# Accumulating transfers of two MLPs issued later: a hold moved to a form's last tile, block sums a group later

## The chip, the cores and the metric

The kernel runs on one core of a Trainium2 chip. The metric is the device time of one execution in microseconds. The core has five engines with a queue of instructions each: TensorE (PE in the profile; its weight loads are PEld), VectorE (DVE), ScalarE (ACT), GpSimd (POOL) and SyncE (SP). SP and POOL also issue the transfers (DMA) between the main memory and the on-chip buffer; an accumulating transfer, which adds what it brings to what lies at its destination, is issued by POOL.

## What is computed

Two layers on a sequence of 512 tokens of width 1024, in float32. Layer 0 has an attention mixer, layer 1 a gated short convolution; behind each stands an MLP with a causal convolution of width 3 between its up projection and its gate.

```python
def conv_ffn(h, norm_g, w_up, conv_w, w_down):      # D_FF = 2816, w_up: 1024 x 5632, w_down: 2816 x 1024
    xn = rms_norm(h, norm_g)
    u = causal_dwconv(xn @ w_up, conv_w)
    g, val = u[..., :D_FF], u[..., D_FF:]
    return (jax.nn.silu(g) * val) @ w_down

def short_conv_mixer(h, norm_g, w_in, conv_w, w_out):
    xn = rms_norm(h, norm_g)
    proj = xn @ w_in
    gate_b, gate_c, u = proj[..., :1024], proj[..., 1024:2048], proj[..., 2048:]
    return (gate_b * causal_dwconv(gate_c * u, conv_w)) @ w_out

for layer in range(2):
    h = h + (attention_mixer if layer % 2 == 0 else short_conv_mixer)(h, ...)
    h = h + conv_ffn(h, ...)
```

## The kernel before

The large products are computed as Strassen-like products of blocks: a product of 2 x 2 blocks takes seven block products, called forms, in place of eight: p1, p7, p2, p6, p3, q5 and q4. Each form multiplies a sum or difference of weight blocks with a sum or difference of activation blocks. Each float32 operand is split into an upper and a lower half (`whi` and `wlo` for weights; ACT rounds the upper one, VectorE subtracts it for the lower one), and three matmuls, hi by hi, lo by hi and hi by lo, give one product.

**Up projections** (class `Sevens`, used for both MLPs and, under the name `c`, for the conv stage's input). The columns are taken in groups `g` of 256. `slot(g, s)` records the work of form `s` of group `g`; the seven slots of a group follow each other. Four blocks of weights, named X, Y, W and Z, are loaded by SP. Sums of them are made by accumulating transfers on POOL (`add_block`): one into X in each group, and in the MLPs one into the tile `three`, which is the operand of forms p6 (before the transfer) and q4 (behind it). X as changed is the operand of q5. `tail(p, s)` does, within the slots of group `g`, the convolution and gate of the group before, `p = g - 1`; in slot 5 it calls `blocks.product`, where VectorE makes the gated activations. These lie in tiles `head_blocks`, `hs_b_blocks` and `hs_a_blocks`, in four quarters a, b, c and d of the down projection's operand. For rows that are complete according to the list `SUMS`, `product` also issues on POOL the block sum, an accumulating transfer within the on-chip buffer that adds quarter a to quarter b (256 or 128 KB).

**Conv stage.** It has groups 0 to 4, of which 1, 2 and 3 are listed in `aside`. In groups 0 and 4 VectorE adds X to Y in place (`first_sums`, kept as `self.summed`); the addition to X on POOL must wait for that, since it changes X. `join` (kept as `self.joined`) subtracts two results on VectorE.

**Down projections** (`mlp`). There are 7 forms by 6 tiles of weights (`GROUPS`: tiles of 2, 2, 2, 1, 2 and 2 blocks of 128 rows), 42 steps in the order p1, p7, p2, p6, p3, q5, q4. `want_sum` lists the tiles, and `bring` issues their transfers, two steps ahead. Tiles of p2 and p3 are plain loads into the three buffers `raw`. Those of the other forms lie in `_chain` tiles: `one(g)` (X_chain, Y_chain, p_hi_chain, p_lo_chain) serves p1 and then q5; `two(g)` (p_hi, p_lo, q_hi, q_lo, q_hi, q_lo with the ending `_chain`) serves p7, p6 and q4 in turn, and the accumulating transfer for the next form can start when the halves of the form before have been split. For q5's last three tiles SP loads a tile `other` into a `raw` buffer and VectorE adds it (line 291).

**What sets the order.** Each queue runs in the order in which it stands. A scheduler places the recorded instructions by their dependences, `pin` (`tc.keep_in_program_order`) keeps an instruction at the place where it was recorded, and `behind(later, earlier)` orders two instructions of one engine. All accumulating transfers stand on POOL's one queue. With an entry in `landed`, `bring` puts a small POOL operation `hold` ahead of a transfer, which reads one column of another tile and so waits until that has landed:

```python
if i in landed:
    hold, other = tiny.tile(...), raws[landed[i]][:, 0:1]
    held_ = pool.tensor_tensor(hold, other, other, op=ALU.add)
    behind(added, held_)
```

The only entry is that of the first MLP (`layer == 0`): the transfer of q4's tile 3 waits for p3's tile 3. Those of tiles 4 and 5 stand behind it.

Of the kernel before, what the change touches and what calls it, by code (L numbers as in the profile page):

```python
# [57 lines left out]
def trunk(  # L58
# [1005 lines left out]
    class Blocks:  # L1064
# [1 line left out]
        SUMS = (0, 2), (2, 4), (4, 6), (6, HEAD), (HEAD, 8), (8, 10), (10, HF)  # L1066

        def __init__(self, place, layer):
            self.layer, self.place, self.parts = layer, place, {}

        def at(self, j, n):
            start = 0 if j < HEAD else HEAD if j < HF else HF
# [9 lines left out]
        def product(self, j, n, g, u):  # L1082
            if n == 2 and j in (HEAD - 1, HF - 1):
                for i in range(2):
                    self.product(j + i, 1, g[:, i:i + 1, :], u[:, i:i + 1, :])
                return
            to = self.at(j, n)
            plus, minus = (LEFT, RIGHT) if j < HF else (RIGHT, LEFT)
            dve.tensor_tensor(to[:, :, plus], g[:, :, plus], u[:, :, plus], op=ALU.mult)
            dve.scalar_tensor_tensor(to[:, :, minus], g[:, :, minus], -1.0, u[:, :, minus], op0=ALU.mult, op1=ALU.mult)  # L1090
            for k0, k1 in self.SUMS:
                if j + n == k1:
                    tc.keep_in_program_order(
                        nc.gpsimd.dma_start(self.block("b", k0, k1 - k0), self.block("a", k0, k1 - k0), accum_op=ALU.add))

    def seven(acc, w, x, fresh, last=True):

# [9 lines left out]
    class Sevens:  # L1107
# [89 lines left out]
        def slot(self, g, s):  # L1197

            on, was, soon = (i in self.groups for i in (g, g - 1, g + 1))
            if self.chores:  # L1200
                self.work_off(self.rate(g, s))
            form, n, fresh = (("p1", "A", True), ("p7", "T", True), ("p3", "R", False), ("p6", "R", False), ("p2", "A", False),
                              ("q5", "R", False), ("q4", "T", False))[s]
            if s == 2:
                if was:
                    self.product(g - 1, form, n, fresh)
            elif on:
                self.product(g, form, n, fresh)
            st, p, c = self.st, g - 1, self.st.get(g)
            if s == 0:  # L1210
                if was:
                    if "p3" not in st[p]:
                        self.weights_of(p, "p3", "Z")
                    self.join(p, "yg", st[p]["T"], st[p]["Xs"])
                if on:
                    self.load_one(g, "W", self.block_of(g, 1, 0))
                if soon:
                    self.load_pair(g + 1)
            elif s == 1:
                first = not was  # L1220
                if on and first and not self.ahead and "p6" not in c:
                    self.weights_of(g, "p6", self.sum_of(g))
                if on and not first and self.table:
                    self.weights_of(g, "p6", "three")
                if on:
                    act.activation(self.bank_of(g, "R"), c["A"], AF.Copy, scale=-1.0)
                if on and not first and not self.table:
                    self.weights_of(g, "p6", self.sum_of(g))
                if on and first and self.name == 0:
                    self.weights_of(g, "p2", "W")  # L1230
                if soon and not self.table:
                    self.add_block(g + 1, "Y", 1, 1)
            elif s == 2:
                if on:
                    self.kept(g, "P7s", c["T"])
                    if "p2" not in c:
                        self.weights_of(g, "p2", "W")
                    c["four"] = c[self.sum_of(g)]
                    if self.table and soon:
                        self.add_block(g, "four", 1, 0)  # L1240
                    else:
                        dve.tensor_tensor(c["four"], c["four"], c["W"], op=ALU.add)
            elif s == 3:
                if was:
                    self.early(p, st[p]["R"])
                if on:
                    self.weights_of(g, "q5", "X")
                    if not self.table:
                        self.kept(g, "Xs", c["R"])
                        self.weights_of(g, "q4", "four")  # L1250
                        self.fourth = self.rest
            elif s == 4:
                if on and self.table:
                    self.kept(g, "Xs", c["R"])
                    self.weights_of(g, "q4", "four")
            if was and s != 2:
                self.tail(p, s)
            if s == 5:
                if on:
                    self.load_one(g, "Z", self.block_of(g, 1, 1))  # L1260
                    self.open_wides(g)
                    if soon and not self.table:
                        self.weights_of(g + 1, "p1", "X")
                        if g + 1 in self.aside:
                            self.three_of(g + 1)
                    self.left(g, c["A"])
                if soon and self.table:
                    self.weights_of(g + 1, "p1", "X")
                elif on and self.ahead and not soon:
                    self.weights_of(g, "p3", "Z")  # L1270
            elif s == 6:
                if on:
                    self.join(g, "yv", c["R"], c["P7s"])
                if soon:
                    self.first_sums(g + 1)
# [17 lines left out]
    def up_begin(layer, norm, mp, place):  # L1293

        blocks = Blocks(place, layer)
        if place is mp:
            blocks.at(0, 1)
        w_up, base = ffn_w_up[layer], PLAIN[layer]

        def block_of(g, kh, half):  # L1300
            c0 = half * DFF + 2 * g * P
            return w_up[kh * 512:(kh + 1) * 512, c0:c0 + 2 * P].rearrange("(k p) c -> p k c", p=P)

        up = Sevens(layer, mp, range(base, HF), block_of)
        up.norm, up.chores = norm, []
        up.table = lambda n, g: table_of(layer, n, g)
        up.scaled = not base
        up.rate = lambda g, s: 1.4 if g == base else 0.3 if layer else 0.5

        def wides_of(g):  # L1310
            if g == base - 1:
                t = hsp.tile([P, 8, S], F32, tag="hs_a", name=f"hs_a_wide{layer}")
                return {n: t[:, 2 * i:2 * i + 2, :] for i, n in enumerate(("yg", "yv", "ug", "uv"))}
            t = {n: mp.tile([P, 2, S], F32, tag=n, name=f"{n}{layer}{g}", bufs=1) for n in ("yg", "yv", "ug", "uv")[0 if place is mp else 2:]}
            if place is not mp:
                both = place.tile([P, 4, S], F32, tag="four", name=f"y_both{layer}{g}")
                t.update(yg=both[:, 0:2, :], yv=both[:, 2:4, :])
            return t
        up.wides_of = wides_of
        wides = up.wides  # L1320

        def taps_of(g, half, i):
            return lambda j: ffn_tap(layer, j, half * NF + 2 * g + i)

        def conv(g, half, i):
            src, dst = (wides[g][n[half]] for n in (("yg", "yv"), ("ug", "uv")))
            causal_conv(dst[:, i, :], src[:, i, :], taps_of(g, half, i))

        def tail(p, s):
            if s < 2:  # L1330
                conv(p, 0, s)
            elif s == 3:
                act.activation(wides[p]["ug"], wides[p]["ug"], AF.Silu)
                conv(p, 1, 0)
            elif s == 4:
                conv(p, 1, 1)
            elif s == 5:
                blocks.product(2 * p, 2, wides[p]["ug"], wides[p]["uv"])
        up.tail, up.conv = tail, conv
        return blocks, up  # L1340

# [230 lines left out]
    def mlp(layer, norm, mp, begun_up=None):  # L1572
# [25 lines left out]
        for name in PHASES:  # L1598
            for g, (k0, nk) in enumerate(GROUPS):
                if name in ("p2", "p3"):  # L1600
                    want_sum(lambda: None, nk, 512, block(1, 0 if name == "p2" else 1, k0, True), queue=pool if name == "p2" and g > 2 else None)
                elif name in ("p1", "q5"):
                    want_sum(
                        one(g), nk, 512, block(0, 0 if name == "p1" else 1, k0, name == "p1"), queue=dve if name == "q5" and g > 2 else None)
                elif name == "p7":
                    want_sum(two(g), nk, 512, block(0, 1, k0, True), block(1, 1, k0, False))
                else:
                    want_sum(two(g), nk, 512, block(0 if name == "p6" else 1, 0, k0, False))
        if layer == 0:
            landed[begun + 6 * len(GROUPS) + 3] = begun + 4 * len(GROUPS) + 3  # L1610
            want_conv()
        else:
            aside.update(range(begun, len(wanted)))
# [251 lines left out]
```

## Time and profile before

| | |
|---|---|
| median of 3 runs | 1103.2 us (1102.69 to 1106.39) |
| profiled execution | 1104.69 us, its span 1102.6 us |
| mean granted TensorE clock | 0.998 |
| busy share | TensorE 99%, its weight loads 93%, VectorE 87%, ScalarE 62%, GpSimd 16% |
| HBM | 205.72 MB read, 44.04 MB written |

The busy share of TensorE comes from matmuls whose ends are modelled and overlap; the number of matmuls that start in a stretch shows more. In rows of busy time by stretch, each engine has its busy us and in brackets its count of instructions (PE, PEld, DVE, ACT, POOL), then the granted clock, the share of the 16 DMA engines and GB/s. In rows in order of time, the columns are start and duration in us, engine, line, operation, written tile and read tiles; in square brackets stands the engine's idle time before it and what ended that. Rows of transfers give count, size and the us from issue to landing.

### The profile page before, as it was taken

The page shows a single profiled execution, that of the slowest core. Times are in us where ns is not written, and L with a number is a line of the kernel's source. Part 1 is how long each engine was busy: PE and PEld are TensorE (multiplying, and loading weights), DVE is VectorE, ACT ScalarE, POOL GpSimd, SP SyncE. Part 2 cuts the span into 40 slices and gives each one's busy share as a digit, 9 for nine tenths or more (in the row PEclk, how much of TensorE's full clock was granted, in tenths as well). Part 3 has the DMA queues.
Part 4 walks back from the last instruction along what each step waited for, and adds up shares of the span by engine and source line. Part 5 has one row for each costly group of instructions (what it writes and reads, how often), then busy time and mean ns, then how long its engine had stood idle before and what let it go on. Part 6 is the DMA issues. An engine that isn't in the chain of part 4 may idle for free.

```text
span 1102.6 us, 21693 instructions
## 1 busy us (share of the span) xinstructions
PE 1086.4 (99%) x8781; PEld 1030.7 (93%) x8781; DVE 959.3 (87%) x1483; ACT 685.3 (62%) x1021; POOL 181.0 (16%) x207
## 2 busy tenths in 40 slices
PE   9999999999999999999999999999999999999998
PEld 7888787879999999999989899999999999999998
DVE  5788898997899788899978889887899999999886
ACT  7466667655466676776546756456566657567653
POOL 4011111111012211114310101001112221014300
PEclk9999999999999999999999999999999999999999
DMA  7677778688667888899963775698879988899951
GB/s 198 166 189 193 187 178 221 173 211 230 190 163 207 198 195 222 210 268 212 232 170 92 193 180 134 135 260 211 212 182 220 209 202 184 222 269 203 240 150 58
DMA packets 178116, 214.21 MB, mean 194 GB/s; under 512 B 7676, under 2 KB 143916, under 8 KB 178016
## 3 DMA queue, kind: packets, MB, share of 16 engines
q0 software_dynamic: 53280, 95.34, 44.7%
q1 hardware_dynamic: 124576, 117.42, 33.4%
q8 instruction: 69, 1.13, 0.4%
q14 instruction: 31, 0.25, 0.1%
q10 hardware_dynamic: 160, 0.07, 0.0%
HBM read 205.72 MB, written 44.04 MB: 227 GB/s over the span
## 4 chain that ended last, share of the span: by engine, by line
PE 66%; DVE 16%; issue 10%; DMA 5%; ACT 3%; POOL 0%; DVEq 0%; ACTq 0%; POOLq 0%
PE psb L357 15%; PE psb L1102 15%; PE psb L1741 7%; PE psa L1741 7%; PE psa L1102 6%; PE psa L357 4%; DMA three<-in_ffn_w_up 4%; DVE wlo_p L1053 3%; DVE wlo L334 2%; PE psb L733 2%; PE psa L830 2%; ACT whi L333 1%; PE psc L357 1%; PE psc L805 1%; PE psb L615 1%
## 5 line engine op out<-in xcount | busy, mean ns | idle before, releaser
L1102 PE MATMUL psb<-p_hi,wlo_p 128*128 128x256 f32 x480 | 132.5, 276 | 1.0 <-DVE wlo_p L74 1.0
L1102 PE MATMUL psb<-p_hi,whi_p 128*128 128x256 f32 x480 | 132.6, 276 | 0.0
L1102 PE MATMUL psb<-p_lo,whi_p 128*128 128x256 f32 x480 | 132.6, 276 | 0.0
L333 ACT ACTIVATE whi<-raw 128x1024 fp32r<-128x1024 f32 (+2 forms) x77 | 79.0, 1027 | 68.7 <-PE psb L357 25.6
L334 DVE TENSOR_TENSOR wlo<-raw,whi 128x1024 fp32r<-128x1024 f32 (+2 forms) x77 | 90.9, 1180 | 24.5 <-ACT whi L333 24.3
L357 PE MATMUL psb<-hs_a,whi 128*128 128x512 f32 (+1 forms) x312 | 93.3, 369 | 0.0
L1102 PEld LDWEIGHTS psb<-p_hi,wlo_p 128*128 128x128 f32 x480 | 90.0, 188 | 1.2 <-DVE wlo_p L74 1.2
L1102 PE MATMUL psb<-q_hi,wlo_q 128*128 128x256 f32 x320 | 89.3, 279 | 1.1 <-DVE wlo_q L1053 1.1
L1102 PEld LDWEIGHTS psb<-p_hi,whi_p 128*128 128x128 f32 x480 | 90.1, 188 | 0.0
L1102 PEld LDWEIGHTS psb<-p_lo,whi_p 128*128 128x128 f32 x480 | 90.1, 188 | 0.0
L1102 PE MATMUL psb<-q_hi,whi_q 128*128 128x256 f32 x320 | 88.9, 278 | 0.8 <-ACT whi_q L1051 0.6
L1102 PE MATMUL psa<-p_hi,wlo_p 128*128 128x256 f32 x320 | 89.3, 279 | 0.2
L1102 PE MATMUL psa<-p_hi,whi_p 128*128 128x256 f32 x320 | 88.5, 277 | 0.0
L1102 PE MATMUL psa<-p_lo,whi_p 128*128 128x256 f32 x320 | 88.5, 277 | 0.0
L1102 PE MATMUL psb<-q_lo,whi_q 128*128 128x256 f32 x320 | 88.5, 277 | 0.0
L357 PE MATMUL psb<-hs_a,wlo 128*128 128x512 f32 (+1 forms) x208 | 69.6, 360 | 0.0
L357 PEld LDWEIGHTS psb<-hs_a,whi 128*128 128x128 f32 x312 | 52.4, 188 | 10.2 <-issue 3.2
L1102 PEld LDWEIGHTS psb<-q_hi,wlo_q 128*128 128x128 f32 x320 | 60.0, 188 | 2.0 <-DVE wlo_q L1053 1.6
L1741 PE MATMUL psb<-act,whi 128*128 128x256 f32 x352 | 60.8, 277 | 0.8 <-DVE act L1055 0.4
L1102 PEld LDWEIGHTS psb<-q_hi,whi_q 128*128 128x128 f32 x320 | 60.1, 188 | 1.6 <-ACT whi_q L1051 0.8
L1102 PEld LDWEIGHTS psa<-p_hi,wlo_p 128*128 128x128 f32 x320 | 60.0, 188 | 1.1 <-DVE wlo_p L1053 0.7
L1102 PEld LDWEIGHTS psa<-p_hi,whi_p 128*128 128x128 f32 x320 | 60.1, 188 | 0.0
(551 smaller groups left out, 3699.5 us busy)
## 6 DMA issues: line engine op xcount, KB each, us to landing
t<-in_ffn_w_up POOLq DMA_DIRECT2D x24, 768.0 KB, 8.0
raw<-in_attn_w_in SPq DMA_DIRECT2D x24, 512.0 KB, 5.5
t<-in_ffn_w_up POOLq DMA_DIRECT2D x12, 1024.0 KB, 10.3
X<-in_ffn_w_up SPq DMA_DIRECT2D x20, 512.0 KB, 5.0
Y<-t SPq DMA_DIRECT2D x20, 512.0 KB, 6.7
three<-t SPq DMA_DIRECT2D x20, 512.0 KB, 5.7
W<-in_ffn_w_up SPq DMA_DIRECT2D x20, 512.0 KB, 3.9
Z<-in_ffn_w_up SPq DMA_DIRECT2D x20, 512.0 KB, 5.4
```

What stands on the lines that cost most here:

```text
L333: return (act.activation(hi_, raw[:, at_], AF.Copy), dve.tensor_tensor(lo_, raw[:, at_], f32(hi_), op=ALU.subtract))
L334: dve.tensor_tensor(lo_, raw[:, at_], f32(hi_), op=ALU.subtract))
L357: made = [pe.matmul(acc[:, c], w[x], rhs[y][:, c], start=first and x + y + c.start == 0, stop=last and x == 1 and c.stop == S) for x, y in ...
L615: pe.matmul(acc, lhs[0], w[0], start=first, stop=False)
L733: pe.matmul(ss[e][:, c:c + wide], ql[rows, b * P:n], kl[rows, 0:wide], start=first and b == bs[0], stop=last and b == bs[-1])
L805: pe.transpose(t[:, k * P:(k + 1) * P], w[:, e, k * P:(k + 1) * P], ident)
L830: pe.matmul(out_, w, t[:, first:first + step * (NB - k - 1) + 1:step, :], start=k == 0 and i == 0, stop=k == NB - 1 and i == 1)
L1053: rest = dve.tensor_tensor(lo, src, f32(hi), op=ALU.subtract)
L1102: pe.matmul(to, w[a][:, k, c], x[b][:, k, :], start=fresh and i + k + t == 0, stop=i == 1 and k == 3 and t == 2, skip_group_check=not fresh)
L1741: pe.matmul(part, l, r[:, c], start=begin and o + t + c.start == 0, stop=end and t == 2 and o + c.start > 0, skip_group_check=not fresh)
```

## The change

There are three edits.

1. `landed` has the same entry in both layers now, and it names p3's tile 5, the last one, in place of tile 3. The second MLP had no hold before.
2. In the first MLP, from its first group in `Sevens` on, `product` only notes the block sums that have come due (`held`), and the next group's slot 5 issues them with `add_up`, ahead of its own product. The second MLP issues them at once as before.
3. In the conv stage, VectorE's join of group 3 is ordered behind the sum of group 4.

```diff
         def __init__(self, place, layer):
-            self.layer, self.place, self.parts = layer, place, {}
+            self.layer, self.place, self.parts, self.sums, self.held = layer, place, {}, [], False
...
-            for k0, k1 in self.SUMS:
-                if j + n == k1:
-                    tc.keep_in_program_order(
-                        nc.gpsimd.dma_start(self.block("b", k0, k1 - k0), self.block("a", k0, k1 - k0), accum_op=ALU.add))
+            self.sums.extend((k0, k1) for k0, k1 in self.SUMS if j + n == k1)
+            if not self.held:
+                self.add_up()
+
+        def add_up(self):
+            for k0, k1 in self.sums:
+                tc.keep_in_program_order(
+                    nc.gpsimd.dma_start(self.block("b", k0, k1 - k0), self.block("a", k0, k1 - k0), accum_op=ALU.add))
+            self.sums = []
...
                     self.join(p, "yg", st[p]["T"], st[p]["Xs"])
+                    if on and not self.table and g not in self.aside:
+                        behind(self.joined, self.summed)
...
             elif s == 5:
+                blocks.add_up()
+                blocks.held = not layer and p < HF - 1
                 blocks.product(2 * p, 2, wides[p]["ug"], wides[p]["uv"])
...
+        landed[begun + 6 * len(GROUPS) + 3] = begun + 4 * len(GROUPS) + 5
         if layer == 0:
-            landed[begun + 6 * len(GROUPS) + 3] = begun + 4 * len(GROUPS) + 3
             want_conv()
```

How the instructions stand, first on POOL in the first MLP's up projection, from the third group of the class on (X and `three` are the additions to weight tiles, the others the block sums). Before:

```order
L1135 DMA X_4055<-in_ffn_w_up 128x4x256
L1135 DMA three_4238<-in_ffn_w_up 128x4x256
L1094 DMA head_blocks_3462<-head_blocks_3462 128x2x256
L1135 DMA X_4272<-in_ffn_w_up 128x4x256
L1094 DMA head_blocks_3462<-head_blocks_3462 128x2x256
L1135 DMA three_4487<-in_ffn_w_up 128x4x256
L1094 DMA head_blocks_3462<-head_blocks_3462 128x256
L1094 DMA hs_b_blocks_4690<-hs_b_blocks_4690 128x256
L1135 DMA X_4521<-in_ffn_w_up 128x4x256
L1135 DMA three_4735<-in_ffn_w_up 128x4x256
```

On the same engine at the same place, after:

```order
L1140 DMA X_4055<-in_ffn_w_up 128x4x256
L1140 DMA three_4238<-in_ffn_w_up 128x4x256
L1140 DMA X_4272<-in_ffn_w_up 128x4x256
L1140 DMA three_4486<-in_ffn_w_up 128x4x256
L1098 DMA head_blocks_3462<-head_blocks_3462 128x2x256 x2
L1140 DMA X_4520<-in_ffn_w_up 128x4x256
L1140 DMA three_4733<-in_ffn_w_up 128x4x256
L1098 DMA head_blocks_3462<-head_blocks_3462 128x256
L1098 DMA hs_b_blocks_4689<-hs_b_blocks_4689 128x256
```

Each block sum has moved behind the next addition to X and the next addition to `three`; the two of 256 KB that stood around X_4272 now stand together behind three_4486.

On POOL in the first MLP's down projection, q4's six transfers with the hold (raw_7037 is p3's tile 3, raw_7104 its tile 5). Before:

```order
L293 DMA p_lo_chain_0_6381<-in_ffn_w_down 128x2x512
L293 DMA q_hi_chain_0_6423<-in_ffn_w_down 128x2x512
L297 TENSOR_TENSOR hold_7413<-raw_7037 128x1
L293 DMA q_lo_chain_0_6457<-in_ffn_w_down 128x512
L293 DMA q_hi_chain_0_6492<-in_ffn_w_down 128x2x512
L293 DMA q_lo_chain_0_6527<-in_ffn_w_down 128x2x512
```

On the same engine at the same place, after:

```order
L293 DMA q_hi_chain_0_6423<-in_ffn_w_down 128x2x512
L297 TENSOR_TENSOR hold_7413<-raw_7104 128x1
L293 DMA q_lo_chain_0_6457<-in_ffn_w_down 128x512
L293 DMA q_hi_chain_0_6492<-in_ffn_w_down 128x2x512
L293 DMA q_lo_chain_0_6527<-in_ffn_w_down 128x2x512
```

Nothing has changed its place; the hold reads the last tile of p3 in place of the fourth. In the second MLP the same hold is new at the same place.

On VectorE in the conv stage, at the start of group 4 (Yc_8506 and Xc_8505 are its Y and X). Before:

```order
L1053 TENSOR_TENSOR wlo_p7c_8696<-Yc_8506,whi_p7c_8695 128x1024
L1162 TENSOR_TENSOR hs_a_conv<-psb_8509,Xsc_8602 128x2x256
L1183 TENSOR_TENSOR Yc_8506<-Yc_8506,Xc_8505 128x1024
L1053 TENSOR_TENSOR wlo_p3c_8727<-Zc_8663,whi_p3c_8726 128x1024
L1053 TENSOR_TENSOR y_8433<-hs_a_conv,y_8433 128x1024
L1493 TENSOR_TENSOR hs_a_conv<-hs_a_conv 128x2x256
```

On the same engine at the same place, after:

```order
L1053 TENSOR_TENSOR wlo_p7c_8696<-Yc_8506,whi_p7c_8695 128x1024
L1188 TENSOR_TENSOR Yc_8506<-Yc_8506,Xc_8505 128x1024
L1053 TENSOR_TENSOR wlo_p3c_8727<-Zc_8663,whi_p3c_8726 128x1024
L1167 TENSOR_TENSOR hs_a_conv<-psb_8509,Xsc_8602 128x2x256
L1053 TENSOR_TENSOR y_8433<-hs_a_conv,y_8433 128x1024
L1502 TENSOR_TENSOR hs_a_conv<-hs_a_conv 128x2x256
```

The join has moved behind the sum and the lower half of p3's weights.

## Prediction

> **What bounds the kernel now.** I read the page's first part, then the busy times by stretch (20 us each, all engines), then the weight loads of TensorE in order of time where a stretch has too few of them, and from there back to what each late operand waited for.
>
> ```profile
> span 1102.6 us, 21693 instructions
> PE 1086.4 (99%) x8781; PEld 1030.7 (93%) x8781; DVE 959.3 (87%) x1483; ACT 685.3 (62%) x1021; POOL 181.0 (16%) x207
> 360.00:380.00 20.00, 18.51 (x154) 17.75 (x154) 13.86 (x19) 10.96 (x14) 4.36 (x4) 1.00 0.77 186
> 380.00:400.00 20.00, 20.00 (x178) 20.00 (x177) 17.58 (x22) 14.96 (x20) 3.82 (x3) 1.00 0.94 218
> 560.00:580.00 20.00, 17.49 (x138) 17.09 (x136) 12.84 (x16) 8.68 (x13) 0.00 (x0) 0.91 0.66 169
> ```
>
> TensorE is the bound: 99% busy, and in a good stretch of the MLPs 178 matmuls of 128x256 start in 20 us, one per 20/178 = 0.112 us. So a change that adds and removes no arithmetic can only win back places where matmuls are missing. The third row lacks 178 - 154 = 24 of them (2.7 us), the fifth 178 - 138 = 40 (4.5 us), and its granted clock is 0.91. These two stretches, in the first MLP's up projection and down projection, are where the change works.
>
> **Block sums a group later (first MLP's up projection).** The stall first, then its cause, in rows of the weight loads, ACT, POOL and the transfers' times to landing:
>
> ```profile
> 372.63 0.19 PEld L1102 LDWEIGHTS psb<-q_hi,whi_q 128*128 128x128 f32 x1 [0.82 <-ACT whi_q L1051]
> 373.89 0.19 PEld L1102 LDWEIGHTS psb<-q_hi,wlo_q 128*128 128x128 f32 x1 [0.96 <-DVE wlo_q L1053]
> 366.08 1.06 ACT L1051 ACTIVATE whi_q<-X 128x1024 fp32r<-128x1024 f32 x1 [1.94 <-DMA X<-in_ffn_w_up]
> 371.52 1.06 ACT L1051 ACTIVATE whi_q<-three 128x1024 fp32r<-128x1024 f32 x1 [2.67 <-DMA three<-in_ffn_w_up]
> 353.94 1.20 POOL L1094 DMA_DIRECT2D head_blocks<-head_blocks  x1 [9.05 <-DVE head_blocks L1090]
> 355.08 1.39 POOL L1135 DMA_DIRECT2D X<-in_ffn_w_up  x1
> 361.66 1.30 POOL L1135 DMA_DIRECT2D three<-in_ffn_w_up  x1 [3.96 <-DVE wlo_p L1053]
> X<-in_ffn_w_up POOLq DMA_DIRECT2D x1, 512.0 KB, 7.2
> X<-in_ffn_w_up POOLq DMA_DIRECT2D x1, 512.0 KB, 11.0
> three<-in_ffn_w_up POOLq DMA_DIRECT2D x1, 512.0 KB, 9.8
> three<-in_ffn_w_up POOLq DMA_DIRECT2D x1, 512.0 KB, 6.3
> ```
>
> TensorE waits for the halves of `three`, these for the accumulating transfer into `three`, issued at 361.66 and landed 9.8 us later. It was slow because the transfers before it were: two block sums of 256 KB lie on either side of the addition to X of 355.08, which took 11.0 us, where the one a group earlier took 7.2. After the change both sums stand behind `three`. Then X's addition has no sum before it and should land near 355 + 7.2 = 362. The addition to `three` has 512 KB of sums behind it in place of ahead. The nearest row for that is the first such addition of this projection, which has one sum of 256 KB issued right behind it: 6.3 us (the last row). Twice that sum, so I allow 6.3 to 8: landed at 368.0 to 369.7. ACT is free for it at 371.52 - 2.67 = 368.85; the lower half ends 0.03 + 1.23 after the upper half's 1.06, so at 371.2 to 372.0, and TensorE wants the first halves at 372.63 - 0.82 - 0.19 = 371.6 and the lower halves two matmuls later. So the stall goes, or 0.3 us of it is left.
>
> What it gives: the idle of the two rows, 0.82 + 0.96 = 1.8, is the lower end where the rest of the missing matmuls is a slow pace that remains; 2.7 is the upper. I take **2.5**, nearer the upper, since the stretch's other missing matmuls follow the same late operands. The sums themselves are read only in the down projection, 100 us later, and the last is issued before it. The five later sums (128 or 256 KB) also move behind a `three`; groups with them run at full rate now (380 to 400), and I cost these moves at nothing, the addition to X being hidden by 11 us from issue to use.
>
> **The hold in the first MLP's down projection.** Names: form p3's weight tiles (`raw`, loaded by SP) come before form q4's accumulating transfers (the `_chain` tiles, on POOL). Rows of TensorE, ACT, POOL, SP, three stretches of 2 us, and landings:
>
> ```profile
> 567.94 0.19 PEld L1741 LDWEIGHTS psa<-act,whi 128*128 128x128 f32 x1 [1.75 <-ACT act L1051]
> 569.28 0.19 PEld L1741 LDWEIGHTS psa<-act,whi 128*128 128x128 f32 x1 [1.16 <-DVE act L1055]
> 559.51 1.06 ACT L333 ACTIVATE whi<-raw 128x1024 fp32r<-128x1024 f32 x1 [1.78 <-PE psa L1741]
> 566.31 1.06 ACT L333 ACTIVATE whi<-raw 128x1024 fp32r<-128x1024 f32 x1 [5.22 <-PE psa L1741]
> 554.68 0.59 POOL L297 TENSOR_TENSOR hold<-raw 128x1 f32<-128x1 f32 x1 [10.92 <-DMA raw<-in_ffn_w_down]
> 556.97 0.37 SPq L300 DMA_DIRECT2D raw<-in_ffn_w_down  x1
> 570.00:572.00 2.00, 2.00 (x11) 2.00 (x10) 2.00 (x3) 0.82 (x2) 0.00 (x0) 0.50 0.76 293
> 572.00:574.00 2.00, 2.00 (x15) 2.00 (x14) 1.90 (x4) 0.28 (x1) 0.00 (x0) 0.69 0.00 0
> 574.00:576.00 2.00, 2.00 (x20) 2.00 (x19) 1.18 (x2) 1.30 (x2) 0.00 (x0) 1.00 0.45 124
> q_lo_chain<-in_ffn_w_down POOLq DMA_DIRECT2D x1, 512.0 KB, 14.0
> other<-in_ffn_w_down SPq DMA_DIRECT2D x1, 512.0 KB, 9.2
> other<-in_ffn_w_down SPq DMA_DIRECT2D x1, 512.0 KB, 3.6
> ```
>
> ACT begins the halves of p3's last tile at 566.31. The profile names TensorE as the releaser, but ACT's cadence is one such operation per 2.7 us (559.51 the one before), so TensorE was done at about 562.2; what came last is the tile, issued by SP at 556.97 and thus 9.3 us under way. Three accumulating transfers of q4 run beside it, the last of them for 14.0 us: the hold let them go at 554.68 + 0.59 = 555.3, when p3's fourth tile had landed. After the change they wait for the last tile. A 512 KB load without them takes 3.6 us (the last row), so that tile lands near 560.6, before ACT can use it. The activation operand then follows as in the steady state, 1.6 to 3 us behind 562.2, in time for TensorE's 566.1.
>
> What it gives: idle 1.75 + 1.16 = 2.9, plus the matmuls at the low clock. Between 570 and 574 there start 11 + 15 in place of 20 + 20 (the counts include overlaps at the edges, the same in each), 14 missing or 1.6 us. Sum 2.9 + 1.6 = **4.5**, as the 20 us stretch has it. Lower end 2.9, if the clock dips all the same. The rows show a clock of 0.50 directly behind the two gaps and 1.00 again four us later, so I count the dip as the stall's. Were it not, this term would be 2.9 (rival B).
>
> The Trainium skill ("TensorE: Matmul & The Clock Gate", Part 1: The HAM clock gate) has it that TensorE falls to half clock after at least one idle window of about 3.4 us. By that rule neither of these gaps is long enough alone, which speaks for B; this trace has the half clock behind gaps of 1.75 and 1.16.
>
> What is late next: the three held transfers now start near 561 and meet SP's `other` tiles (512 KB issued at 561.86, the next after p3's last tile is split, about 562.2 + 1.06 + 1.23 = 564.5). Rows of that issue, of its addition on VectorE, and of ACT's first use of a held transfer:
>
> ```profile
> 561.86 0.37 SPq L290 DMA_DIRECT2D other<-in_ffn_w_down  x1
> 578.12 1.22 DVE L291 TENSOR_TENSOR p_hi_chain<-p_hi_chain,other 128x1024 f32<-128x1024 f32 x1
> 592.31 0.62 ACT L333 ACTIVATE whi<-q_lo_chain 128x512 fp32r<-128x512 f32 x1
> ```
>
> Moved up by 4.5 the first is at 573.6, 11.7 us after its tile's issue; beside such transfers that tile took 9.2 (row above). So 2.5 us to spare. The held transfers are first needed at 592.31 - 4.5 = 587.8; started at 561.4, with the 14.0 us of the slowest, they land by 576. POOL has nothing else queued behind them here.
>
> **The hold in the second MLP's down projection, and the conv stage's order.**
>
> ```profile
> 1060.77 0.30 PEld L1741 LDWEIGHTS psa<-whi,act 128*128 128x128 f32 x2 [0.23 <-ACT act L1051]
> 1061.51 0.30 PEld L1741 LDWEIGHTS psa<-wlo,act 128*128 128x128 f32 x2 [0.44 <-DVE wlo L334]
> 1062.11 0.54 PEld L1741 LDWEIGHTS psa<-whi,act 128*128 128x128 f32 x4 [0.30 <-DVE act L1055]
> 1059.13 1.06 ACT L333 ACTIVATE whi<-raw 128x1024 fp32r<-128x1024 f32 x1 [1.84 <-DMA raw<-in_ffn_w_down]
> 705.16 1.22 DVE L1183 TENSOR_TENSOR Yc<-Yc,Xc 128x1024 f32<-128x1024 f32 x1
> 706.91 1.28 POOL L1135 DMA_DIRECT2D Xc<-in_conv_w_in  x1 [18.36 <-issue]
> 715.78 1.06 ACT L1051 ACTIVATE whi_q5c<-Xc 128x1024 fp32r<-128x1024 f32 x1 [5.16 <-DMA Xc<-in_conv_w_in]
> 717.37 0.19 PEld L1102 LDWEIGHTS psb<-q_hic,whi_q5c 128*128 128x128 f32 x1 [0.37 <-ACT Xsc L1169]
> 718.15 0.19 PEld L1102 LDWEIGHTS psb<-q_hic,wlo_q5c 128*128 128x128 f32 x1 [0.48 <-DVE wlo_q5c L1053]
> ```
>
> In the second MLP nothing is held now, and the same tile comes 1.84 us late to ACT; TensorE loses 0.23 + 0.44 + 0.30 = 1.0. The hold adds one POOL operation of 0.59 us (554.68) on an engine with nothing else to do there, and takes the 1.0 away if the held transfers do no harm later. Ends: a gain of 1.0, and a loss of 1.0 if they delay the `other` tiles instead; I take **-0.9**. In the conv stage the sum on VectorE stands ahead of a join of 0.6 us (the step from the join's start at 704.56 to 705.16), so the addition to Xc that follows is issued 0.6 earlier, and of the 0.37 + 0.48 that TensorE waits for it, **0.6** goes. The join comes two operations later, 1.2 + 1.1 us; the operation that followed the three keeps its time, so its users do too. Ends: 0 and 0.85.
>
> **Sum.** 2.5 + 4.5 + 0.9 + 0.6 = 8.5 us. The profiled execution took 1104.69 us (span 1102.6 and 2.1 around it), 1.5 above the median 1103.2. It goes to 1096.2; seen from the median, to **1094.7**.
>
> **Rivals.** (A) The sums behind `three` slow it, or the X addition stays slow since W, X and Y of the next group load at 351.7 to 353: the up stall stays, -6.0, 1097.2. For it: `three` has no more than 0.3 us to spare at the upper end. Against: 6.3 us beside a sum. (B) The clock dips in any case: -6.9, 1096.3; against it the rows above. (C) The first MLP's last p3 tile is still late, or the `other` tiles take its place, and the 4.5 turns into 0 to 1: -4 to -5, 1098.7. It speaks for it that six transfers, 2.5 MB with the `other` tiles, must still move between 557 and 576. (D) The hold does not bite, since another semaphore already kept the transfers that long: only 2.5 + 0.6 are won, 1100.1. Against it: they left at 555.3, straight behind the hold. (E) Slower: the held transfers go ahead of the `other` tiles as a block. At 14.0 us from 561.86 the first `other` lands at 575.9, 2.3 after its need; its addition is next in VectorE's fixed order, so all operands queue behind it, the second adds 0.9, and a dip of the clock 1.6: 4.8 in the first MLP eats the 4.5, and as much in the second, with no gain there, gives -8.5 + 4.8 + 0.9 + 4.8 = +2, 1105.2. It is slower by over 0.3% where `other` takes some 15 us or more, 1.3 / 2 beyond 14.0; beside the same three transfers it took 9.2.
>
> **How the numbers follow.** The forecast (1092 to 1096) has 0.60, A 0.13, B 0.06, C 0.12, D 0.05, E 0.04. The range 1092.4 to 1099.2: the forecast's upper ends are 2.7 + 4.5 + 1.0 + 0.85 = 9.05, 1094.1, and below that 0.5 for the runs' spread under the median and 1.2 for short waits further on that may hang on the same transfers; above, it takes in A, B and most of C. About 0.3%, or 3.3 us, is what a measurement of this kernel can tell from no change: faster 0.84 (the forecast, A, B and part of C), same 0.11, slower 0.05.
>
> **What the changed profile would show.** Right: the stretch that holds the fourth group's q4 slot has some 178 matmuls and no wait of 0.8 for `whi_q`; the hold in the first MLP ends near 561, ACT's last p3 halves begin near 562 less what was won before, and no stretch has a clock under 1.00 there; p3 in the second MLP has no waits on ACT or VectorE. Wrong: an X or `three` addition of 10 us again; VectorE's additions of `other` idle behind a DMA; the wait for p3's last tile still there with the POOL transfers later.

## The result, and the profile after

The changed kernel took 1097.5 us (median of 5 runs, 1096.71 to 1099.15) against 1105.89 us (median of 5, 1102.69 to 1108.1) of the kernel before: the ratio is 0.9931, with a 95% interval of 0.9908 to 0.9954. Run again beside 30 runs of the kernel before it came to 0.9941 (0.9922 to 0.9959). So it is faster by 6 to 8 us. The forecast was 1094.7 us: a sum of 8.5 taken from 1103.2, the median of the first 3 runs. The time lies within the range, but above the forecast's own (1092 to 1096), near the number of rival A. It was not rival A, as the profile shows.

The profiled execution took 1097.78 us. From the first part of its page:

```profile
span 1096.0 us, 21688 instructions
PE 1082.0 (99%) x8781; PEld 1027.7 (94%) x8781; DVE 959.6 (88%) x1483; ACT 685.8 (63%) x1021; POOL 183.5 (17%) x208
```

Its busy times by stretch, columns as before:

```profile
360.00:380.00 20.00, 20.00 (x179) 20.00 (x178) 17.84 (x24) 13.87 (x19) 5.04 (x4) 1.00 1.00 228
560.00:580.00 20.00, 19.35 (x171) 19.15 (x170) 16.68 (x20) 11.82 (x17) 2.24 (x2) 1.00 0.88 211
840.00:860.00 20.00, 18.26 (x156) 17.73 (x156) 16.76 (x23) 11.97 (x15) 2.90 (x3) 1.00 0.80 183
```

The last stretch in the kernel before:

```profile
840.00:860.00 20.00, 20.00 (x179) 20.00 (x179) 18.97 (x25) 12.75 (x17) 3.78 (x3) 1.00 0.90 207
```

The stretch of the up stall (the waits for `three` near 372) has its 179 matmuls, where it had 154; the down stretch has 171 where it had 138, at a clock of 1.00 in place of 0.91. But in the second MLP's up projection something new stands: 840 to 860 had 179 matmuls before and has 156 now.

To see where the time went I matched the weight loads of the two traces, which stand in the same order in both, and took after minus before of their starts (the median over 3 us, at times of the kernel before). Where this lag falls, time is won; where it rises, time is lost:

```
at us    340   385   550   640   700   722   820   870   1040   1080
lag us   0.0  -2.9  -2.9  -7.5  -7.5  -8.6  -8.4  -5.0   -5.3   -6.5
```

So 2.9 are won in the first MLP's up projection, 4.6 in its down projection, 1.1 in the conv stage and 1.3 in the second MLP's down projection, 9.9 in all. Between 820 and 870, 3.4 are lost again. The span fell by 6.6.

The up stall, in rows of POOL and ACT in order of time:

```profile
355.32 1.29 POOL L1140 DMA_DIRECT2D X<-in_ffn_w_up  x1 [10.38 <-DVE wlo_p L1053]
361.90 1.28 POOL L1140 DMA_DIRECT2D three<-in_ffn_w_up  x1 [5.30 <-DVE wlo_p L1053]
367.77 1.06 ACT L1051 ACTIVATE whi_q<-three 128x1024 fp32r<-128x1024 f32 x1 [0.89 <-DMA three<-in_ffn_w_up]
```

And the two transfers, us from issue to landing at the end:

```profile
X<-in_ffn_w_up POOLq DMA_DIRECT2D x1, 512.0 KB, 7.3
three<-in_ffn_w_up POOLq DMA_DIRECT2D x1, 512.0 KB, 5.8
```

Both were issued when they were before, but landed after 7.3 and 5.8 us in place of 11.0 and 9.8. ACT splits `three` at 367.77, where it was 371.52.

The first MLP's hold, in rows of POOL, ACT and VectorE in order of time:

```profile
557.94 1.00 POOL L297 TENSOR_TENSOR hold<-raw 128x1 f32<-128x1 f32 x1 [16.60 <-DMA raw<-in_ffn_w_down]
559.29 1.06 ACT L333 ACTIVATE whi<-raw 128x1024 fp32r<-128x1024 f32 x1 [1.14 <-PE psa L1750]
560.19 2.05 POOL L293 DMA_DIRECT2D q_lo_chain<-in_ffn_w_down  x1
570.68 1.22 DVE L291 TENSOR_TENSOR p_hi_chain<-p_hi_chain,other 128x1024 f32<-128x1024 f32 x1
```

And the last of the three held transfers to its landing:

```profile
q_lo_chain<-in_ffn_w_down POOLq DMA_DIRECT2D x1, 512.0 KB, 11.4
```

ACT takes p3's last tile at 559.29, straight behind TensorE's release and a step of 2.72 behind the tile before. The hold bites: the transfers leave at 558.9, 3.6 us later than before, though the work around them runs 2.9 earlier; the slowest took 11.4 us in place of 14.0. VectorE's addition of `other` does not wait for its tile.

The new stall, in rows of TensorE's weight loads, ACT, POOL and VectorE:

```profile
857.95 0.19 PEld L1107 LDWEIGHTS psb<-q_hi,whi_q 128*128 128x128 f32 x1 [1.18 <-ACT whi_q L1051]
859.21 0.19 PEld L1107 LDWEIGHTS psb<-q_hi,wlo_q 128*128 128x128 f32 x1 [0.96 <-DVE wlo_q L1053]
856.85 1.06 ACT L1051 ACTIVATE whi_q<-three 128x1024 fp32r<-128x1024 f32 x1 [3.91 <-DMA three<-in_ffn_w_up]
849.19 1.29 POOL L1140 DMA_DIRECT2D three<-in_ffn_w_up  x1 [7.04 <-DVE ug L466]
847.25 1.22 DVE L1053 TENSOR_TENSOR wlo_p<-three,whi_p 128x1024 fp32r<-128x1024 f32 x1
```

The addition of 849.19 to its landing:

```profile
three<-in_ffn_w_up POOLq DMA_DIRECT2D x1, 512.0 KB, 7.6
```

The VectorE and POOL rows of the kernel before, where TensorE did not wait, and that addition to its landing:

```profile
854.64 1.22 DVE L1053 TENSOR_TENSOR wlo_p<-three,whi_p 128x1024 fp32r<-128x1024 f32 x1
856.16 1.29 POOL L1135 DMA_DIRECT2D three<-in_ffn_w_up  x1 [6.62 <-DVE wlo_p L1053]
three<-in_ffn_w_up POOLq DMA_DIRECT2D x1, 512.0 KB, 5.6
```

It looks like the stall that the first MLP lost: ACT waits for the addition to `three`. Yet the addition is not slow because of sums ahead of it. POOL waits for the end of VectorE's `wlo_p<-three` and starts the addition 856.16 - 855.86 = 0.30 behind it before, and 849.19 - 848.47 = 0.72 behind it now (the late issue, below); and it then takes 7.6 us to land in place of 5.6. The bracket of the row at 849.19 names VectorE's `ug` in place of `wlo_p<-three`, since `ug` ended last, at 849.12. But 0.07 behind is less than the 0.29 that any other addition to `three` takes at the least, and in the program of either kernel POOL waits for the same operation, `wlo_p<-three`. The order of every queue in this projection is the same in both kernels. That became the question of the experiments.

### The profile page after: what moved, and what is told of

Same layout as the page of the kernel before. It is cut to its first block, busy times and chain, and to the rows that moved or that the text cites. A ratio compares the mean times of both kernels' runs of the same rounds, so it can differ in the third digit from the quotient of the medians.

```text
span 1096.0 us, 21688 instructions
## 1 busy us (share of the span) xinstructions
PE 1082.0 (99%) x8781; PEld 1027.7 (94%) x8781; DVE 959.6 (88%) x1483; ACT 685.8 (63%) x1021; POOL 183.5 (17%) x208
## 4 chain that ended last, share of the span: by engine, by line
PE 71%; DVE 12%; issue 9%; DMA 5%; ACT 2%; POOL 0%; SPq 0%; DVEq 0%; POOLq 0%; ACTq 0%
PE psb L1107 16%; PE psb L357 15%; PE psb L1750 9%; PE psa L1750 8%; PE psa L1107 6%; PE psa L357 4%; DMA three<-in_ffn_w_up 3%; DVE wlo_p L1053 2%; PE psb L733 2%; PE psa L830 2%; DVE wlo L334 1%; PE psc L357 1%; PE psc L805 1%; PE psb L615 1%; DMA Xc<-in_conv_w_in 1%
```

## The experiments

All times are medians; the kernel before took 1105.0 to 1105.9 us beside them. "Lag" is the difference of matched weight loads, as above, against the changed kernel run again.

| kernel | us (runs) | ratio to before, 95% |
|---|---|---|
| changed, again | 1098.91 (9) | 0.9941 (0.9922 to 0.9959) |
| sums at once | 1099.62 (10) | 0.9949 (0.9929 to 0.9968) |
| first hold at fourth tile | 1102.71 (12) | 0.9974 (0.9950 to 0.9997) |
| sums held in both MLPs | 1099.63 (12) | 0.9953 (0.9937 to 0.9968) |
| second MLP without hold | 1099.12 (6) | 0.9942 (0.9923 to 0.9962) |
| join first | 1100.33 (12) | 0.9960 (0.9945 to 0.9976) |
| before, short sums | 1102.9 (12) | 0.9976 (0.9960 to 0.9992) |
| hold at fifth tile | 1098.91 (6) | 0.9943 (0.9924 to 0.9961) |
| two POOL instructions more | 1099.41 (10) | 0.9960 (0.9943 to 0.9977) |
| four more | 1098.86 (11) | 0.9953 (0.9937 to 0.9969) |
| before, two fewer | 1103.28 (12) | 0.9994 (0.9972 to 1.0015) |
| late issue | 1102.29 (12) | 0.9976 (0.9959 to 0.9994) |

**The changed kernel again.**

> The changed kernel as it is, once more, beside the three kernels that undo or extend a part. If its traces repeat, it takes 1096 to 1099 us and the second MLP's up projection again loses 3 us at about 858 (wait of 1.18 for whi_q, window 840 to 860 with some 156 matmuls). If that new stall was chance in one execution, the window has some 178 and the time is near 1094.5.

1098.91 us, and the new stall is there again (waits of 0.98 and 0.96, 159 matmuls in 840 to 860, the addition issued 0.73 behind its VectorE operation and landed after 7.4). It is no chance of one execution.

**Sums at once.** The second edit undone; the first and the third stay.

```diff
-                blocks.held = not layer and p < HF - 1
+                blocks.held = False
```

> The changed kernel with the block sums issued at once in the first MLP too; the three other edits stay. Theory: the sums ahead of X and three delay these, so the wait for whi_q near 372 comes back, the stretch 360 to 380 falls to some 154 matmuls, and the time is the changed kernel's plus 2.6 (1100). Rival: the sums don't matter, and X and three landed sooner by luck: the stretch keeps 178 and the time stays within 0.5 of the changed kernel's.

Busy times of two stretches of this kernel:

```profile
360.00:380.00 20.00, 18.28 (x154) 17.68 (x154) 14.32 (x19) 11.80 (x16) 4.35 (x4) 1.00 0.80 192
840.00:860.00 20.00, 20.00 (x175) 19.73 (x174) 18.82 (x26) 12.68 (x16) 3.79 (x3) 1.00 0.85 198
```

The second MLP's fifth addition to `three`, and the operation that it waits for:

```profile
849.76 1.22 DVE L1053 TENSOR_TENSOR wlo_p<-three,whi_p 128x1024 fp32r<-128x1024 f32 x1
851.28 1.28 POOL L1140 DMA_DIRECT2D three<-in_ffn_w_up  x1 [6.62 <-DVE wlo_p L1053]
```

The same transfer to its landing:

```profile
three<-in_ffn_w_up POOLq DMA_DIRECT2D x1, 512.0 KB, 6.0
```

Half of the theory came true: 154 matmuls again, and a lag of 2.9 behind the stall. But the second MLP's stall has gone (issue 0.30 behind, landing after 6.0 us, 175 matmuls), and by 870 the lag is -0.7. The expected 2.6 came to 0.7 in the medians, which the spread of the runs does not tell from nothing. So what the held sums win in the first MLP comes back, nearly whole, as a stall in the second, whose own instructions they don't touch.

Not all of the 3.4 lost between 820 and 870 is this stall. Its two waits are 2.1. Against the same profile of before, three kernels without the late issue (this one, and the short sums and two fewer below) lose 0.9 to 1.7 there too: that profile has no wait of 0.2 in 840 to 880, and was a good draw in this place.

**First hold at the fourth tile.** The first edit undone in the first MLP.

```diff
-        landed[begun + 6 * len(GROUPS) + 3] = begun + 4 * len(GROUPS) + 5
+        landed[begun + 6 * len(GROUPS) + 3] = begun + 4 * len(GROUPS) + (5 if layer else 3)
```

> The changed kernel with the first MLP's hold back at p3's fourth tile; the second MLP's hold stays at the last tile. Theory: the three transfers leave 4 us sooner, p3's last tile lands some 9 us after its issue, TensorE waits twice (1.75 and 1.16) near 565, the clock dips, and the time is the changed kernel's plus 4.5 (1102). Rival B: the dip of the clock is a thing of its own, and the hold is worth 2.9 alone (1100.4). Rival C: what comes behind was shifted by the earlier edits, and the fourth tile costs 0 to 1 (1098).

The stretch of the down stall:

```profile
560.00:580.00 20.00, 17.59 (x153) 17.20 (x152) 13.93 (x18) 9.77 (x14) 0.00 (x0) 1.00 0.57 157
```

Its weight loads that waited:

```profile
564.18 0.19 PEld L1750 LDWEIGHTS psa<-act,whi 128*128 128x128 f32 x1 [1.64 <-ACT act L1051]
565.53 0.19 PEld L1750 LDWEIGHTS psa<-act,whi 128*128 128x128 f32 x1 [1.16 <-DVE act L1055]
```

Both waits are back and the median rises by 3.8, so it is not rival C. In the profiled execution the clock stayed at 1.00, and the lag behind the waits is 3.0, the idle time alone, as rival B had it; 0.3 come at q5 (a wait of 1.16 in place of 0.85). The medians can't tell the theory's 4.5 from B's 2.9, for its 12 runs lie between 1097.8 and 1106.4, where the 9 of the changed kernel span 2.5 us. The price of the fourth tile thus changes from one execution to the next: the four profiles of kernels with it (before, this one, short sums, two fewer) have 3.0 to 5.3 by the lag, three of them with a dip of the clock, and 4.5 was one draw. That the spread of the runs is this price, and that it can be smaller or larger than these four, is likely but not shown.

**Sums held in both MLPs.**

```diff
-                blocks.held = not layer and p < HF - 1
+                blocks.held = p < HF - 1
```

> The changed kernel with the block sums of the second MLP issued a group later as well. Theory: the new stall at 858 in the second MLP's up projection is the one that the first MLP had at 372, by the same sums ahead of the addition to X: it goes, the window 840 to 860 has some 178 matmuls in place of 156, and the time falls by about 3 (1094.5). Rival: the transfer into three was slow there for another reason (it was issued with the DMA engines nearly idle), and the wait stays: 1097.5. Third: the sums now behind three delay three, and the stall moves by some microseconds with the same loss.

The stretch of the second MLP's stall:

```profile
840.00:860.00 20.00, 18.27 (x152) 17.87 (x151) 16.78 (x24) 11.38 (x15) 3.68 (x3) 0.96 0.81 171
```

A weight load three groups later:

```profile
918.26 0.19 PEld L1107 LDWEIGHTS psb<-q_hi,whi_q 128*128 128x128 f32 x1 [1.29 <-ACT whi_q L1051]
```

The stall stays (the issue is 0.72 behind again), so the second MLP's own sums don't cause it; the rival stands. The third case came as well, elsewhere: the addition to `three` of 908.88 has a held sum behind it and takes 8.3 us, where it takes 5.9 to 7.2 in the other profiles, and a wait of 1.29 follows.

**Second MLP without the hold.** The entry in `landed` only where `layer == 0`.

> The changed kernel without the hold in the second MLP's down projection. Theory: the last p3 tile is 1.8 late to ACT near 1052 again, TensorE waits three times for 0.2 to 0.45, and the time is the changed kernel's plus 0.9 to 1.6 (1098.4 to 1099). Rival: these waits were those of one execution, and nothing changes (within 0.3).

The weight load that waits in the second MLP's p3:

```profile
1057.30 0.53 PEld L1750 LDWEIGHTS psa<-whi,act 128*128 128x128 f32 x4 [0.30 <-DVE act L1055]
```

One short wait comes back and the lag goes from -0.3 to +0.3 there, but the median is only 0.2 above, within the spread: rather the rival. Short sums and two fewer (below), which hold nothing in the second MLP either, have no wait of 0.15 or more there. So the waits of 0.23, 0.44 and 0.30 in the profile of before were one draw, and this hold is worth less than their sum.

**Join first.** The two lines of the third edit taken out.

> The changed kernel with the conv stage's order undone (the join of Xs stands ahead of the sum again). Theory: the addition to Xc is issued 0.6 later, the waits of 0.37 and 0.48 near 710 come back, and the time is the changed kernel's plus 0.5 to 1.1 (1098 to 1098.6). Rival: the waits hang on what loads beside Xc, not on the 0.6, and nothing changes.

The weight loads of the conv stage that wait:

```profile
709.44 0.19 PEld L1107 LDWEIGHTS psb<-q_hic,whi_q5c 128*128 128x128 f32 x1 [0.31 <-ACT Xsc L1174]
710.22 0.19 PEld L1107 LDWEIGHTS psb<-q_hic,wlo_q5c 128*128 128x128 f32 x1 [0.48 <-DVE wlo_q5c L1053]
```

Both waits are back, and the lag goes from 0.0 to 0.7 at them, as the theory has it. The four profiles without this order have 0.79 to 0.86 of such waits, the ten with it 0 to 0.36. The median rises by 1.4; where the rest is, its profile (of its fastest run) does not show.

**Short sums.** The kernel before, with each of the first MLP's sums cut to a sixteenth of its columns, at its old place in the queue; it leaves out the rest of these additions.

> The kernel before, with the first MLP's block sums cut to 16 of 256 columns, in the same places of the POOL queue with the same waits; this leaves out 15/16 of the addition of these blocks. Theory (bytes): it is the sums' 512 KB that slow the additions to X and three, so the wait for whi_q near 372 goes although the order is as before, and the time is 1103.2 - 2.6 = 1100.6. Rival (queue): it is the sums' own wait for VectorE on the POOL queue that makes X's addition late; then the wait near 372 stays and the time is 1103.

The stretch of the up stall:

```profile
360.00:380.00 20.00, 20.00 (x179) 20.00 (x178) 17.52 (x23) 14.48 (x19) 5.01 (x5) 1.00 0.90 208
```

The transfers of POOL around it (the last row is the two short sums):

```profile
X<-in_ffn_w_up POOLq DMA_DIRECT2D x1, 512.0 KB, 7.3
three<-in_ffn_w_up POOLq DMA_DIRECT2D x1, 512.0 KB, 5.9
head_blocks<-head_blocks POOLq DMA_DIRECT2D x2, 16.0 KB, 6.4
```

With the order as before, the additions land as fast as in the changed kernel, the stall is gone and the median falls by 2.9 (2.7 by the ratio, with an interval of 0.9 to 4.4). It is the 512 KB of the two sums that slowed them, and not their place in POOL's queue. There is no stall in the second MLP (174 matmuls in 840 to 860, 0.30 at the issue).

**Hold at the fifth tile**, in both MLPs (`+ 4` for `+ 5`).

> The changed kernel with the hold at p3's fifth tile in both MLPs, between the fourth and the last. Theory: what counts is how much of the three transfers runs beside the last tile; they leave some 2.5 us sooner than in the changed kernel, the last tile lands 1 to 4 us later, and of the 4.5 about half is lost: 1099 to 1100. Rival: the fifth tile is late enough, and the time is the changed kernel's (within 0.5).

The first MLP's hold, and then the stretch with the end of p3:

```profile
554.87 1.22 POOL L297 TENSOR_TENSOR hold<-raw 128x1 f32<-128x1 f32 x1 [14.43 <-DMA raw<-in_ffn_w_down]
```

```profile
550.00:570.00 20.00, 20.00 (x179) 20.00 (x178) 17.67 (x24) 11.26 (x16) 4.53 (x4) 1.00 0.83 210
```

The transfers leave 2.3 us earlier than in the changed kernel run again, and nothing is lost: the rival. The last tile of p3 needs a head start, not the queue to itself.

**Where the late issue comes from.** The issue 0.72 to 0.74 behind stands in the profile of each kernel so far with the sums held in the first MLP, and 0.30 in each without. The fifth addition to `three` is instruction 279 of POOL's program in the former (277 with the sums held in both MLPs), and 281 in the latter, since moved sums need two semaphore waits fewer. I took the place in POOL's instruction stream for the cause and shifted it. Two (here) or four more instructions at POOL's start, and two fewer in the kernel before, where VectorE sets `ones` and a part of `begin` in place of POOL:

```diff
     pool.memset(ones, 1.0)
+    pool.memset(ones, 1.0)
+    pool.memset(ones, 1.0)
```

> The changed kernel with two idle instructions more on POOL at its very start (the memset of a 128x1 constant done three times). All runs so far with the sums held issue one addition to three, the fifth of the second MLP, 0.72 us behind the VectorE operation that it waits for, where the same instruction elsewhere starts 0.30 behind it, and lose some 3 us to a wait for whi_q behind it; those with the sums at once don't. In the program it is POOL's instruction 279 there (277 with both MLPs held), and 281 in the kernels without the delay, since other semaphore waits are needed where the sums stand elsewhere. Theory (place in POOL's instruction stream): two instructions more make it 281 again, the issue comes 0.30 behind, the wait near 858 is gone, the window 840 to 860 has some 178 matmuls, and the time is 1098.9 - 3 = 1096. Rival (queue or descriptor state left by the order of the transfers): the instructions change nothing of that, the 0.72 and the wait stay, 1099.

> The changed kernel with four idle instructions more on POOL at its start (the addition is its instruction 283). Theory (place in the stream): the delay falls on a semaphore wait that has long been met, or on another instruction; if it is hidden the time is 1096, as with two more. If it falls on another addition of the second MLP, that one starts 0.72 behind its operation and a wait of TensorE stands there: 1096 to 1099. Rival: as the changed kernel, the delay at the same addition, 1099.

> The kernel before with two constants set by VectorE in place of POOL at the start, so that the same addition is POOL's instruction 279 without any change of the sums or holds. Theory (place in the stream): the addition near 856 is now issued 0.72 behind its VectorE operation, TensorE waits near 865 as in the changed kernel, and the time is that of before plus 2.5 to 3: 1108.5. Rival (it is the order of the sums' transfers): 0.30 as before, and 1105.8.

The addition and its VectorE operation in the changed kernel with two more, and then in the kernel before with two fewer:

```profile
848.37 1.22 DVE L1055 TENSOR_TENSOR wlo_p<-three,whi_p 128x1024 fp32r<-128x1024 f32 x1
850.32 1.29 POOL L1142 DMA_DIRECT2D three<-in_ffn_w_up  x1 [7.04 <-DVE ug L468]
```

```profile
855.79 1.22 DVE L1053 TENSOR_TENSOR wlo_p<-three,whi_p 128x1024 fp32r<-128x1024 f32 x1
857.31 1.28 POOL L1135 DMA_DIRECT2D three<-in_ffn_w_up  x1 [6.63 <-DVE wlo_p L1053]
```

0.73 and 0.30, as without the shift; with four more 0.73. The stall at 859 stays with two and with four more, and the kernel before with two fewer has no wait above 0.41 there. My theory falls in all three runs. What the profiles with the late issue share, and the others lack, is the moved sums in the first MLP, 480 us earlier, with the semaphore waits that changed with them. Which of the two it is, and how it reaches this far, is not shown.

**Late issue.** Does a late issue by itself make the stall? The kernel with the sums at once, which has none, with one POOL operation ahead of this one addition:

```diff
+            if self.name == 1 and g == 4 and n == "four":
+                v = self.st[g][n][:, 0, 0:1]
+                tc.keep_in_program_order(pool.tensor_scalar(v, v, 1.0, None, op0=ALU.mult))
```

> The kernel with the sums at once in both MLPs and both holds (which has no wait near 858), with one idle operation on POOL ahead of one transfer: a multiplication by 1.0 of one column of the tile three of the second MLP's fifth group, which has to wait for the same VectorE operation as the addition to that tile, so that this addition is issued some 0.4 to 0.8 us later and nothing else is. Theory: such a delay by itself makes the addition land 1.5 us later, since SP's load of the next three runs beside more of it, and TensorE then waits for whi_q near 860: window 840 to 860 or 860 to 880 with some 156 matmuls, and the time 1099.6 + 2.5 = 1102. Rival: the late issue and the wait of the kernels with held sums both come from something else, a delay of 0.4 is covered, the window keeps 174 or more, and the time is within 0.7 of 1099.6.

Rows of POOL, and the weight load that waits:

```profile
851.70 1.78 POOL L1142 TENSOR_SCALAR three<-three 128x1 f32<-128x1 f32 x1 [6.42 <-DVE wlo_p L1053]
853.78 1.32 POOL L1143 DMA_DIRECT2D three<-in_ffn_w_up  x1 [0.30 <-POOL three L1142]
861.57 0.19 PEld L1107 LDWEIGHTS psb<-q_hi,whi_q 128*128 128x128 f32 x1 [1.67 <-ACT whi_q L1051]
```

The stretch behind it:

```profile
860.00:880.00 20.00, 17.71 (x150) 17.21 (x150) 18.01 (x25) 11.96 (x15) 4.34 (x4) 1.00 0.81 182
```

The operation took 1.78 us, so the issue stands 853.78 - 851.59 = 2.2 behind in place of 0.30, more than I meant. The stall appears, the lag against the kernel without it grows by 2.6 there, and the ratio rises by 0.0027, 3.0 us (the intervals of the two ratios still overlap; the trace decides). So an issue 2 us late is enough for such a stall. That 0.42 is enough is not shown by this run, nor is the way that was expected: SP's load of the next `three` went 0.36 ahead of the addition here, and the addition landed after 6.6 us, little slower than 6.0. In the changed kernel the 0.42 comes with a landing 1.6 us slower (7.6 against 6.0), so the addition lands about 2 us later in all. There SP's load of the next `three` is issued 1.1 us behind the addition, against 1.5 with the sums at once, and runs beside more of it; that this slows the landing is argued only.

No version beat the changed kernel by more than the spread; holding at the fifth tile equals it.

## Why the prediction was right, and where it was wrong

**Term 2.5, block sums.** Right in mechanism and size at its place: 2.9 by the lag, X landed after 7.3 (7.2 forecast), `three` after 5.8 (6.3 to 8). That the bytes of the sums do it, short sums showed. Wrong is the step that ended the account there: the second MLP issues its sums at once as before, and so its up projection has no term in the sum. The trace loses 3.4 there between 820 and 870, some 2 to 2.5 of it in the new stall, and the kernel with the sums at once, which keeps the other edits, is only 0.7 slower than the changed kernel. The second edit is worth 0.7 or so, if anything, and not 2.5, because of a wait that no list of moved instructions shows.

**Term 4.5, the hold.** Right in mechanism: 4.6 by the lag, 3.8 in the medians when undone. The working took one execution for the price. It also left out the first of SP's three `other` tiles, of 256 KB and issued at 558.85, ahead of the one of 561.86; no harm came of that. The claim "the dip as the stall's" holds halfway: in 14 profiles no stretch between 320 and 1080 has a clock under 1.00 without a pair of waits in it or right ahead of it, but of the 17 pairs with both waits at 0.9 or more 9 brought a dip and 8 did not. Waits of 0.94 and 0.96 did with two POOL instructions more and did not with the join first; 1.64 and 1.16 did not. So the waits come with the dip, but don't settle it, and where none came the place cost the idle time alone, as rival B has it. By the idle window of about 3.4 us in the Trainium skill ("TensorE: Matmul & The Clock Gate", Part 1: The HAM clock gate) no pair here should bring a half clock, since no wait is that long; the dips behind waits of 0.95 and 0.96 speak against it.

**Term 0.9, the second hold.** Mis-sized: 1.3 by the lag of the two traces, but 0.2 in the medians and 0.6 by the lag when undone, and two profiles without this hold have no such wait at all. The profile of before, with 1.0 of waits, was again one draw.

**Term 0.6, the join.** 1.1 by the lag, 0.7 when undone: right, if a little small.

**Sum.** 8.5 forecast; the four places gave 9.9, and the place without a term took 3.4. That the time still fell inside the range is in part luck: the places gave 1.4 more than forecast, which made up for some of the loss. The start was too low besides. The median of before rose from 1103.2 to 1105.89 with two more runs, and from there the sum of 8.5 gives 1097.4, where 1097.5 was measured; but the gain itself is 6 to 8, not 8.5.

**Rivals.** A is excluded by the 179 matmuls, though its number came out. C is excluded by ACT's row at 559.29. D by the hold's row. E by VectorE's addition at 570.68, 3 us sooner than the 573.6 that I had allowed.

## What to carry to other kernels

Undo an edit as well as look at its place: the stall it removed was gone as forecast, and only the kernel without the edit showed that nearly all of it had been paid back later. A place that waits for late transfers can have a price that changes from one execution to the next; its gap in one profile is a sample, so look at the spread of the runs before a term is taken from it. Where a transfer on the path lands late beside others, take bytes from beside it, and look at what lies beside the place that they are moved to: the same sums held in the second MLP too slowed another addition.

## What the runs showed of the hardware that was not expected

- With the reordering of transfers on POOL's queue near 360 us goes a change of when one addition starts near 849 us: 0.72 to 0.74 behind the operation it waits for in the nine profiles with the sums held, 0.30 in four of the five others (in the fifth, the late issue, the added operation starts 0.11 behind). Other additions change with it: with the sums held the one to X near 758 starts 0.52 behind, where it is 0.30 without; the one to `three` near 402 is 0.55 behind without, and 0.30 with. Instruction counts on POOL don't change it. What ties these together is open.
- All four kernels with the first hold at the fourth tile have runs spread over 7 to 10 us (1099.4 to 1109.3 for 30 runs of the kernel before); the others spread over 1.7 to 5.7.
- A POOL operation on a 128x1 column took 1.78 us in the late issue; the first MLP's hold, another of that shape, took 0.59 before, 1.00 after and 1.22 at the fifth tile.
